# A two-layer attention trunk: when the sums for the output weights are taken, when the gates are scaled, and which engine splits the outputs

## The chip, the cores and the metric

The kernel runs on one core of one Trainium2 chip. The core has five engines with queues of their own: TensorE (PE, matrix products and transposes, with the loading of weights counted apart as PEld), VectorE (DVE), ScalarE (ACT), GpSimd (POOL) and SyncE (SP), which here issues every DMA. The metric is the device time of one launch in microseconds; the time of a kernel is the median of its runs.

## The reference, cut to what matters

A trunk of two layers over 1024 tokens of width 1024, 16 heads of 64, float32:

```python
for i in range(2):
    h = rmsnorm(x, norm_g[i])
    # layer 0: forgetting attention (causal, with a bias from cumulated log-gates)
    # layer 1: native sparse attention (compressed + selected blocks + sliding window, gated)
    o, z = mixer(h)                       # z is 1024 columns of the same input projection
    x = x + (o * silu(z)) @ w_out         # the output projection
out = rmsnorm(x, final_g)
```

What the change touches lies around the last line of the loop: the gate silu(z), the product with o, and the projection by W_out.

## The kernel before, in words

**Numbers.** TensorE multiplies in pairs of halves: a value is split into a high part and a rest (hi, lo), and a product is three matmuls, hi·hi, hi·lo, lo·hi (`mm3`, lines 256 to 258). The output projections do this in float16, so their operands are first scaled by powers of two. The scales come from bounds: a sum of squares of all of W_out, and for each pair of heads a sum of squares of z with a bound of v.

**Squares.** `Squares` (lines 160 to 187) holds a list of weight pieces. One `step` takes the square of the piece that was loaded last (ScalarE, L183, with its sum over each row) and then issues the load of the next (SyncE, L173). A tiny ScalarE operation (L182, tile `zg`) ties the step to some tile that has just been made, so that it comes at that place in the order. In layer 0 (`early`, one buffer) the steps stand behind each half of the k, v, q and z sections, and two behind each finished pair of the pairs 0 to 5. The list is 40 pieces of layer 1's input weights, then the gate weights (column 40 of `sums`), then 16 pieces of layer 0's W_out (columns 49 to 64).

**Order of the work.** Each layer runs two Python generators that `merge` interleaves by costs they yield: the main one is attention (scores, exponentials, transposes, products with v), the fill one is projections. Where one yields a function, it stands still until that condition holds. The order so traced is the priority of the instructions in each engine's queue; each engine then runs its own queue in order, and waits on semaphores for others.

In layer 0, `fox_fill` makes the sections k, v, q, z for eight pairs of heads, each section 8 steps of three 128x512 matmuls for each half of the tokens. `fox_main` works through duos of row blocks; the last duo of a pair calls the tail of `FoxDuo.finish`: transpose o (L793), multiply with the scale of the pair and z (L795), copy to float16 (ScalarE, L801), take the rest (GpSimd, L802), store (SyncE, L806). Pair 7 keeps its outputs on chip. In its turn in the fill come z, the second half of q, then `out_scales` (some 14 VectorE operations of a few elements, two ScalarE casts and two small matmuls, through `roots`), then the load of half of W_out, the first half of q, and the split of the rows. `load_wout16` splits W_out in pieces of 128x512: ScalarE makes the high part (L682); of every two pieces the rest of one is made by VectorE (L684) and of the other by GpSimd in two operations (L686, L687).

The scale of a pair in layer 0 is five VectorE operations on one column behind the second half of z (L574 to L577, with `half_root`, L222 and L224). In layer 1 it is seven (L1453 to L1459). `ready["c", p]` holds it.

In layer 1, `nsa_zs` is the fill: eight z sections of float16 matmuls, `out_scales`, the split of W_out, and products of finished pairs (`out_start`). The main part, `run_attn`, works through 32 `NsaSuper` (16 heads, two halves of the queries). For the window part of each, GpSimd makes the high half and the rest of the probabilities (L1628, L1629) and a transposing DMA (L1631) follows; the chosen blocks are transposed by TensorE (L1647) and split by ScalarE and VectorE (L273, L274). `close` does for layer 1 what the tail of `finish` does for layer 0 (L1704 to L1715).

At the end of either layer the rest of the fill runs as products only.

Of the kernel before, what the change touches and what calls it, by code (L numbers as in the profile page):

```python
# [21 lines left out]
P = 128  # L22
# [19 lines left out]
def tile_fox_nsa(ctx, tc, a, out):  # L42
# [409 lines left out]
    def fox_k(p):  # L452
        KH = [sk.tile([P, S], F32R, tag="KH", name=f"KH_{p}_{j}") for j in range(2)]
        KL = [sk.tile([P, S], F32R, tag="KL", name=f"KL_{p}_{j}") for j in range(2)]
        w = next_w() if p else wq.pop(0)
        for half in range(2):
            ts = slice(half * 512, half * 512 + 512)
            pt = ps_a(f"k{p}_{half}")
            yield from project(w, hT, half, pt)
            for j in range(2):  # L460
                r, o = rows[j], rows[1 - j]
                A.copy(KH[j][r, ts], pt[r, :])
                V.tensor_tensor(KL[j][r, ts], pt[r, :], f(KH[j][r, ts]), OP.subtract)
                dma(f(KH[j][o, ts]), f(KH[j][r, ts]))
                dma(f(KL[j][o, ts]), f(KL[j][r, ts]))
            yield 0
            if p:
                early.step(pt[:, 0:1])
        ready["k", p] = KH, KL
# [92 lines left out]
    def fox_z(p, w, halves=(1, 0)):  # L562
        zs = ready.setdefault(("zt", p), {})
        if not ao:
            ao.append(sb[0].tile([P, 8], F32, name="ao0", bufs=1))
        zq = sb[0].tile([P, 6], F32, tag="zq", bufs=3, name=f"zq_{p}")
        for half in halves:
            pt = ps_a(f"z{p}_{half}")
            yield from project(w, hT, half, pt)
            zs[half] = z = sb[0].tile([P, 512], F32, tag="z", bufs=4, name=f"z_{p}_{half}")  # L570
            A.activation(z, pt, AF.Square, accum_out=zq[:, half:half + 1])
            silu2(z, pt)
            if half == 0:
                V.tensor_tensor(zq[:, 2:3], zq[:, 0:1], zq[:, 1:2], OP.add)  # L574
                half_root(zq, 2)
                V.tensor_scalar(zq[:, 5:6], zq[:, 4:5], 2.0 ** 46, None, OP.mult)
                V.scalar_tensor_tensor(ao[0][:, p:p + 1], zq[:, 3:4], 2.0 ** 81, ready["v", p][1], OP.mult, OP.mult)  # L577
                ready["c", p] = zq[:, 5:6]
            ready["z", p, half] = zs
            early.step(z[:, 0:1])  # L580

    early = Squares(sa, [(a["nsa_w"][i][:, 4 * x:4 * x + 4, :], 2 * n + x)
                         for n, i in enumerate((*range(12), *range(20, 28))) for x in range(2)]
                    + [(a["nsa_w_g"].rearrange("(k p) c -> p k c", p=P), 40)] + row_sets(a["fox_w_out"], 512, 49), 512, 1)
    un0 = consts.tile([P, 12], F32, name="un0")
    ao = []
    first = []
# [1 line left out]
    def fox_fill():  # L589
        for p in range(8):  # L590
            if p >= 2:
                yield lambda p=p: ("scored", p - 2) in ready
            yield from k0 if p == 0 else fox_k(p)
            if p == 0:
                for _ in range(11):
                    yield next(gate0)
            if p >= 2:
                yield lambda p=p: ("done", p - 2) in ready
            yield from fox_v(p)
            if p == 0:  # L600
                yield from gate0
                sb.append(tc.alloc_tile_pool(name="sb", bufs=2, reuse_waits="tile"))
            if p < 7:
                yield from fox_q(p, next_w())
                yield from fox_z(p, next_w())
                if p == 6:
                    first.append(roots(sums[:, 0:41], ((0, 4), (4, 8), (8, 24), (24, 40), (40, 41)), "early"))
            else:
                wq, wz = next_w(), next_w()
                yield from fox_z(p, wz)  # L610
                yield from fox_q(p, wq, (1,))
                assert not early.items and not early.at
                ready["wscale"], ready["undo"] = out_scales(ao[0], sums[:, 49:65], "o0", un0, sb[0])
                rows0 = load_wout16(hp, "fox_w_out", 1, 200)
                yield next(rows0)
                yield from fox_q(p, wq, (0,))
                yield from rows0
                ready["o7"] = hp.tile([P, NT, 2, P], F16, tag="h11", name="o7_0")
                yield from out_start0(load_wout16(hp, "fox_w_out", 0, 200))

# [43 lines left out]
                load(n + 1)  # L664
                yield 1000

    def load_wout16(pool, src, half, pace, scale=None):


        lo = pool.tile([P, 4, D], F32, tag=f"h{half}1", name=f"wos_{src}_{half}")  # L670
        for k in range(4):
            r = 4 * (1 - half) + k
            dma(lo[:, k, :], a[src][r * P:(r + 1) * P, :])
        yield 0
        w = pool.tile([P, 2, 4, D], F16, tag=f"h{half}0", name=f"wo_{src}_{half}")
        for k in range(4):
            r = 4 * (1 - half) + k
            sc = ready["wscale"][:, r:r + 1]
            for c in range(2):
                yield pace  # L680
                cs = slice(c * 512, c * 512 + 512)
                A.activation(w[:, 0, k, cs], lo[:, k, cs], AF.Copy, scale=sc)  # L682
                if c:
                    V.scalar_tensor_tensor(w[:, 1, k, cs], lo[:, k, cs], sc, w[:, 0, k, cs], OP.mult, OP.subtract)  # L684
                else:
                    G.tensor_scalar(lo[:, k, cs], lo[:, k, cs], sc, 1.0, OP.mult, OP.mult)  # L686
                    G.tensor_tensor(w[:, 1, k, cs], lo[:, k, cs], w[:, 0, k, cs], OP.subtract)  # L687
        ready.setdefault("wout", []).append((w[:, 0], w[:, 1]))
# [7 lines left out]
    class FoxDuo:  # L696
# [78 lines left out]
        def finish(self):  # L775
# [10 lines left out]
            if j == 1 and x == 3:  # L786
                ready["done", p] = True
                for s in (1, 0):
                    yield lambda s=s: ("z", p, s) in ready
                    yield 1000  # L790
                    pt = ps_t(f"pto_{p}_{s}")
                    for i in range(4):
# [5 lines left out]
                    else:  # L798
                        ot = o[:, 4 * s:4 * s + 4].bitcast(F16).rearrange("p t (x q) -> p t x q", x=2)
                    z4 = z.rearrange("p (t q) -> p t q", t=4)  # L800
                    A.copy(ot[:, :, 0], z4)  # L801
                    G.tensor_tensor(ot[:, :, 1], z4, ot[:, :, 0], OP.subtract)  # L802
                    if p < 6:
                        early.step(z[:, 0:1])
                    if p < 7:
                        dma(oF[0][p * P:(p + 1) * P, 4 * s:4 * s + 4], ot)  # L806
                    ready["o", p, s] = True
# [615 lines left out]
    def limits():  # L1423
# [12 lines left out]
        V.tensor_scalar(b[:, 1].bitcast(I32), b[:, 0].bitcast(I32), 0x7F800000, None, OP.bitwise_xor)  # L1436
        ready["limits"] = b[:, 1]

    def nsa_z(p, w, halves=(1, 0)):
        if p == 0:  # L1440
            limits()
# [3 lines left out]
        zq = zs["q"]  # L1445
        for half in halves:
            pt = ps_a(f"nz{p}_{half}")
            yield from project(w, hT, half, pt)
            zs[half] = z = pers.tile([P, 512], F32, tag="z", bufs=4, name=f"nz_{p}_{half}")
            A.activation(z, pt, AF.Square, accum_out=zq[:, half:half + 1])  # L1450
            silu2(z, pt, ready["units"][2])
            if half == 0:
                V.tensor_tensor(zq[:, 2:3], zq[:, 0:1], zq[:, 1:2], OP.add)  # L1453
                half_root(zq, 2)
                V.tensor_scalar(zq[:, 5:6], zq[:, 4:5], 2.0 ** 74, None, OP.mult)
                V.tensor_tensor(zq[:, 6:7], zq[:, 5:6], ready["limits"][:, p // 2:p // 2 + 1], OP.mult)
                V.tensor_scalar(zq[:, 6:7], zq[:, 6:7], 2.0 ** 100, None, OP.min)
                V.tensor_scalar(zq[:, 7:8].bitcast(I32), zq[:, 6:7].bitcast(I32), 0x7F800000, None, OP.bitwise_xor)
                V.tensor_scalar(ao1[:, p:p + 1], zq[:, 7:8], 0.5, None, OP.mult)  # L1459
                ready["c", p] = zq[:, 6:7]  # L1460
                ready["z", p, 1] = zs
            if half == 0:
                ready["z", p, 0] = zs
            ready["v"] = True

    def nsa_zs():
        for p in range(8):
            if p == 6:
                rows0 = load_wout16(h1, "nsa_w_out", 1, 400)
                yield next(rows0)  # L1470
            if p >= 2:
                yield lambda p=p: ("done", p - 2) in ready
            yield from nsa_z(p, zw[p])
        assert not late.items and not late.at
        ready["wscale"], ready["undo"] = out_scales(ao1, late.out, "o1", pers.tile([P, 12], F32, name="un1"), pers)
        yield from rows0
        ready["o7"] = h1.tile([P, NT, 2, P], F16, tag="h11", name="o7_1")
        yield from out_start(load_wout16(h1, "nsa_w_out", 0, 400))

    class Halves:  # L1480

# [78 lines left out]
    class NsaSuper:  # L1560
# [134 lines left out]
        def close(self):  # L1695
# [2 lines left out]
            if h % 2 == 0:  # L1698
                return
            o, t = self.O[p, s], self.O[p, s, "t"]  # L1700
            yield lambda: ("z", p, s) in ready
            pt = ps_t(f"ptn_{self.name}")
            for qi in range(4):
                T.transpose(pt[:, qi * P:(qi + 1) * P], t[:, qi, :], ident)  # L1704
# [152 lines left out]
```

## Time and profile before

| | us |
|---|---|
| median of three runs | 1472.32 (1471.29 to 1477.2) |
| the profiled execution's own time | 1477.65 |
| its span, from first to last instruction | 1475.8 |
| TensorE busy | 1371.1 (93%) |
| VectorE busy | 1112.8 (75%) |
| ScalarE busy | 924.5 (63%) |
| GpSimd busy | 594.2 (40%) |

Layer 0 runs to about 620 us of the span (with its last products to about 655), the first part of layer 1 (projections, compressed attention, block choice) to about 980, sparse attention to about 1410, the end to 1476. A row of a wait view reads: who waited, for which engine and line, total us, times, the longest. A row of a group reads: line, engine, operation, tile out and in, shapes, count, then busy us and mean ns of one, then the engine's idle time before them and what ended it. A row of a tile view gives minimum, median and maximum ns and the first and last start in us.

### The profile page before, as it was taken

To read this page: it belongs to the slowest core of one execution; us is meant where nothing else is said; L and a number is where in the kernel's file an instruction comes from. 1 tells how busy PE (TensorE), PEld (TensorE's weight loads), DVE (VectorE), ACT (ScalarE), POOL (GpSimd) and SP (SyncE) were. 2 spreads that over 40 slices of the span, in tenths; PEclk is the share of its full clock that TensorE was granted. 3 is DMA by queue.
4 is the path that set the end of the run, shared out by engine and by line. 5 is a ranking of instruction groups with operands and counts; after the bars stand their busy time and mean duration, and the time that the engine had idled before them with its cause. 6 is when DMAs were issued, how large, how long until landed. Compare 5 with 4: busy or idle time off the path is not lost. (4 is left out here: it accounts for less than half of the span.)

```text
span 1475.8 us, 30392 instructions
## 1 busy us (share of the span) xinstructions
PE 1371.1 (93%) x10499; PEld 931.0 (63%) x10499; DVE 1112.8 (75%) x3010; ACT 924.5 (63%) x2344; POOL 594.2 (40%) x785
## 2 busy tenths in 40 slices
PE   5999999999999989989999988879999999988998
PEld 4878877877777755444545544447666766655643
DVE  6586677776868788586757667878989999888834
ACT  5376767676776564255555476657877878778612
POOL 2233333323332352121202456235766766669500
PEclk9999999999999999999999999999999999999999
DMA  5388788887988898546464446445667686774633
GB/s 200 90 174 187 186 186 198 193 187 190 188 197 169 162 260 193 118 154 198 140 222 124 152 110 164 121 137 100 123 147 167 134 175 123 145 173 100 120 113 143
DMA packets 414923, 234.73 MB, mean 159 GB/s; under 512 B 334448, under 2 KB 372656, under 8 KB 414768
## 3 DMA queue, kind: packets, MB, share of 16 engines
q1 hardware_dynamic: 414768, 232.78, 66.5%
q8 instruction: 83, 1.36, 0.4%
q14 instruction: 72, 0.59, 0.1%
HBM read 120.31 MB, written 28.38 MB: 101 GB/s over the span
## 5 line engine op out<-in xcount | busy, mean ns | idle before, releaser
L1614 PE MATMUL S_n<-nk,nq 128*128 128x320 f16 (+5 forms) x768 | 156.8, 318 | 17.4 <-DVE m_n L1622 16.1
L755 ACT ACTIVATE P<-P,m 128x512 f32<-128x512 f32 (+1 forms) x192 | 116.3, 607 | 56.3 <-DVE m L746 55.5
L1629 POOL TENSOR_TENSOR hl_n<-P_n,hl_n 128x640 f16<-128x640 f32 (+4 forms) x128 | 143.8, 1123 | 10.0
L757 DVE SCALAR_TENSOR_TENSOR hl<-P,hl 128x512 f16<-128x512 f32 (+1 forms) x192 | 115.3, 616 | 41.2 <-ACT hl L756 39.9
L726 POOL TENSOR_TENSOR Bd<-B,tri 128x128 f32<-128x128 f32 x128 | 61.6, 498 | 203.0 <-DVE m L746 187.0
L1628 POOL CAST hl_n<-P_n 128x640 f16<-128x640 f32 (+4 forms) x128 | 76.8, 600 | 116.2 <-ACT P_n L1625 91.5
L1625 ACT ACTIVATE P_n<-P_n,m_n 128x640 f32<-128x640 f32 (+7 forms) x128 | 98.5, 770 | 32.2 <-DVE m_n L1622 31.3
L1625 ACT ACTIVATE P_n<-P_n,m_n,units 128x640 f32<-128x640 f32 (+4 forms) x128 | 100.1, 783 | 28.7 <-DVE m_n L1624 25.6
L1614 PEld LDWEIGHTS <-nq 128*128 128x128 f16 x768 | 71.8, 99 | 63.7 <-issue 27.3
L273 ACT ACTIVATE pth_n<-ptp_n 128x512 f16<-128x512 f32 (+1 forms) x160 | 85.4, 545 | 40.4 <-PE ptp_n L1647 39.1
L274 DVE SCALAR_TENSOR_TENSOR ptl_n<-ptp_n,pth_n 128x512 f16<-128x512 f32 (+1 forms) x160 | 99.9, 633 | 11.1 <-ACT pth_n L273 8.8
L1647 PE MATMUL ptp_n<-ident,P_n 128*128 128x128 f32 x576 | 94.3, 281 | 5.3 <-DVE un L238 1.7
L756 ACT ACTIVATE hl<-P 128x512 f16<-128x512 f32 (+1 forms) x192 | 92.6, 512 | 2.0 <-ACT P L755 0.4
L1622 DVE CUSTOM_DVE_ANT_0 P_n<-S_n,wmask 128x640 f32<-128x640 f32 (+4 forms) x128 | 83.2, 650 | 9.0 <-PE S_n L1614 8.8
L183 ACT ACTIVATE sq<-sq,zg 128x512 f32<-128x512 f32 (+2 forms) x73 | 59.5, 815 | 39.7 <-DMA sq<-in_nsa_w_dram 24.8
L1647 PEld LDWEIGHTS ptp_n<-ident,P_n 128*128 128x128 f32 x576 | 66.3, 143 | 27.5 <-DVE ptl_n L274 9.3
L1622 DVE CUSTOM_DVE_ANT_0 P_n<-S_n,bias,units 128x640 f32<-128x640 f32 (+1 forms) x64 | 68.8, 1075 | 4.6 <-PE S_n L1614 4.6
L771 PE MATMUL O<-v,pT 128*128 128x128 f16 x576 | 59.4, 223 | 13.7 <-DMA pT<-hl 9.8
L1655 PE MATMUL O_n<-nv,pth_n 128*128 128x64 f16 x576 | 71.7, 193 | 0.2
L1656 PE MATMUL O_n<-nv,pth_n 128*128 128x64 f16 x576 | 71.7, 193 | 0.0
L737 PE MATMUL S<-KH,Q 128*128 128x512 f32 (+1 forms) x192 | 66.3, 360 | 3.7 <-DVE m L746 2.2
L1657 PE MATMUL O_n<-nv,ptl_n 128*128 128x64 f16 x576 | 68.8, 193 | 0.3 <-DVE ptl_n L274 0.3
(522 smaller groups left out, 4707.2 us busy)
## 6 DMA issues: line engine op xcount, KB each, us to landing
sq<-in_nsa_w_dram SPq DMA_DIRECT2D x40, 256.0 KB
B<-cD SPq DMA_DIRECT2D x16, 512.0 KB
nq<-qD SPq DMA_DIRECT2D x64, 128.0 KB
x<-in_x_dram SPq DMA_DIRECT2D x8, 512.0 KB
wst_k<-in_fox_w_dram SPq DMA_DIRECT2D x8, 512.0 KB
wst_v<-in_fox_w_dram SPq DMA_DIRECT2D x8, 512.0 KB
wst_q<-in_fox_w_dram SPq DMA_DIRECT2D x8, 512.0 KB
KH<-KH SPq DMA_DIRECT2D x32, 128.0 KB
```

Of the source, the lines that this page charges most:

```text
L273: A.activation(hi[:, 0:n], pt[:, 0:n], AF.Copy, scale=scale)
L274: V.scalar_tensor_tensor(lo[:, 0:n], pt[:, 0:n], scale, h, OP.mult, OP.subtract)
L755: A.activation(L[:, 0:n], L[:, 0:n], AF.Exp, bias=init, scale=-1.0, accum_out=self.lr[:, col + c:col + c + 1])
L756: A.activation(hi[:, cs], L[:, 0:n], AF.Copy, scale=UP)
L757: V.scalar_tensor_tensor(lo[:, cs], L[:, 0:n], UP, hi[:, cs], OP.mult, OP.subtract)
L1614: T.matmul(ps[:, b, 0:w], self.q[x][:, qi * P:(qi + 1) * P], k[:, k0 + b * w:k0 + b * w + w], start=(x == 0), stop=(x == 1))
L1622: V.tensor_tensor_reduce(dst, src, mk, 1.0 if y else unit, 3e38, OP.add, OP.min, m)
L1625: A.activation(L, L, AF.Exp, bias=m, scale=minus if y else -1.0, accum_out=self.l[:, y, qi:qi + 1])
L1628: G.tensor_copy(hl[:, 0:n], L)
L1629: G.tensor_tensor(hl[:, n:2 * n], L, hl[:, 0:n], OP.subtract)
L1647: T.transpose(pt[:, (x + i) * P:(x + i + 1) * P], L[:, kb * P - k0:(kb + 1) * P - k0], ident)
L1655: T.matmul(o, hi, v[:, 0:64], start=first, stop=False)
```

## The change

1. `early` takes the 16 pieces of W_out before the gate weights, and no longer has steps behind finished pairs. Its last step now stands behind the last half of the last pair's q.
2. The scale of pair p in layer 0 moves into `z_scale`, called behind the first half of pair p+1's k section; for pair 7 behind the second half of q. `finish` waits for the scale instead of z.
3. In layer 0's last pair `out_scales` moves behind the load of W_out's rows and four steps of the first half of q; the roots of layer 1's weights move from the end of pair 6 to behind the split of the rows.
4. The float16 copy in `finish` moves from ScalarE to GpSimd.
5. In layer 1 the scale moves into `nz_scale`, called four steps into the next pair's z section, for pair 7 behind a pause of 2000 cost units; `out_scales` follows it. `close` waits for the scale.
6. In layer 1 `load_wout16` gets `gp=False`: the rests are all made by VectorE.

```diff
@@ fox_k
             yield from project(w, hT, half, pt)
+            if p and half == 0:
+                z_scale(p - 1)
@@ fox_z (nsa_z likewise loses its seven operations at half 0)
             silu2(z, pt)
-            if half == 0:
-                V.tensor_tensor(zq[:, 2:3], zq[:, 0:1], zq[:, 1:2], OP.add)
-                half_root(zq, 2)
-                V.tensor_scalar(zq[:, 5:6], zq[:, 4:5], 2.0 ** 46, None, OP.mult)
-                V.scalar_tensor_tensor(ao[0][:, p:p + 1], zq[:, 3:4], 2.0 ** 81, ready["v", p][1], OP.mult, OP.mult)
-                ready["c", p] = zq[:, 5:6]
...
+    def z_scale(p):
...
@@ early
-                    + [(a["nsa_w_g"].rearrange("(k p) c -> p k c", p=P), 40)] + row_sets(a["fox_w_out"], 512, 49), 512, 1)
+                    + row_sets(a["fox_w_out"], 512, 49)
+                    + [(a["nsa_w_g"].rearrange("(k p) c -> p k c", p=P), 40)], 512, 1)
@@ fox_fill
-                if p == 6:
-                    first.append(roots(sums[:, 0:41], ..., "early"))
             else:
                 wq, wz = next_w(), next_w()
                 yield from fox_z(p, wz)
                 yield from fox_q(p, wq, (1,))
-                ready["wscale"], ready["undo"] = out_scales(ao[0], sums[:, 49:65], "o0", un0, sb[0])
+                z_scale(p)
                 rows0 = load_wout16(hp, "fox_w_out", 1, 200)
                 yield next(rows0)
-                yield from fox_q(p, wq, (0,))
+                last_q = fox_q(p, wq, (0,))
+                for _ in range(4):
+                    yield next(last_q)
+                ready["wscale"], ready["undo"] = out_scales(ao[0], sums[:, 49:65], "o0", un0, sb[0])
+                yield from last_q
                 yield from rows0
+                first.append(roots(sums[:, 0:41], ..., "early"))
@@ load_wout16
-                if c:
+                if c or not gp:
                     V.scalar_tensor_tensor(w[:, 1, k, cs], lo[:, k, cs], sc, w[:, 0, k, cs], OP.mult, OP.subtract)
@@ FoxDuo.finish
-                    yield lambda s=s: ("z", p, s) in ready
+                    yield lambda: ("c", p) in ready
...
-                    A.copy(ot[:, :, 0], z4)
+                    G.tensor_copy(ot[:, :, 0], z4)
                     G.tensor_tensor(ot[:, :, 1], z4, ot[:, :, 0], OP.subtract)
-                    if p < 6:
-                        early.step(z[:, 0:1])
@@ nsa_z
+            steps = project(w, hT, half, pt)
+            if half and p:
+                for _ in range(4):
+                    yield next(steps)
+                nz_scale(p - 1)
+            yield from steps
@@ nsa_zs
-                rows0 = load_wout16(h1, "nsa_w_out", 1, 400)
+                rows0 = load_wout16(h1, "nsa_w_out", 1, 400, False)
...
+        yield 2000
+        nz_scale(7)
         ready["wscale"], ready["undo"] = out_scales(ao1, late.out, ...)
...
-        yield from out_start(load_wout16(h1, "nsa_w_out", 0, 400))
+        yield from out_start(load_wout16(h1, "nsa_w_out", 0, 400, False))
@@ NsaSuper.close
-            yield lambda: ("z", p, s) in ready
+            yield lambda: ("c", p) in ready
```

More of the change, by code (lines that the diff above doesn't have):

```diff
@@ L565, in fox_z @@
             ao.append(sb[0].tile([P, 8], F32, name="ao0", bufs=1))
-        zq = sb[0].tile([P, 6], F32, tag="zq", bufs=3, name=f"zq_{p}")
+        zs["q"] = zq = sb[0].tile([P, 6], F32, tag="zq", bufs=3, name=f"zq_{p}")
         for half in halves:
@@ L572, in fox_z @@
             silu2(z, pt)
-            if half == 0:
-                V.tensor_tensor(zq[:, 2:3], zq[:, 0:1], zq[:, 1:2], OP.add)
-                half_root(zq, 2)
-                V.tensor_scalar(zq[:, 5:6], zq[:, 4:5], 2.0 ** 46, None, OP.mult)
-                V.scalar_tensor_tensor(ao[0][:, p:p + 1], zq[:, 3:4], 2.0 ** 81, ready["v", p][1], OP.mult, OP.mult)
-                ready["c", p] = zq[:, 5:6]
             ready["z", p, half] = zs
             early.step(z[:, 0:1])
+    def z_scale(p):
+        zq = ready["zt", p]["q"]
+        V.tensor_tensor(zq[:, 2:3], zq[:, 0:1], zq[:, 1:2], OP.add)
+        half_root(zq, 2)
+        V.tensor_scalar(zq[:, 5:6], zq[:, 4:5], 2.0 ** 46, None, OP.mult)
+        V.scalar_tensor_tensor(ao[0][:, p:p + 1], zq[:, 3:4], 2.0 ** 81, ready["v", p][1], OP.mult, OP.mult)
+        ready["c", p] = zq[:, 5:6]
     early = Squares(sa, [(a["nsa_w"][i][:, 4 * x:4 * x + 4, :], 2 * n + x)
                          for n, i in enumerate((*range(12), *range(20, 28))) for x in range(2)]
-                    + [(a["nsa_w_g"].rearrange("(k p) c -> p k c", p=P), 40)] + row_sets(a["fox_w_out"], 512, 49), 512, 1)
+                    + row_sets(a["fox_w_out"], 512, 49)
+                    + [(a["nsa_w_g"].rearrange("(k p) c -> p k c", p=P), 40)], 512, 1)
     un0 = consts.tile([P, 12], F32, name="un0")
@@ L605, in fox_fill @@
                 yield from fox_z(p, next_w())
-                if p == 6:
-                    first.append(roots(sums[:, 0:41], ((0, 4), (4, 8), (8, 24), (24, 40), (40, 41)), "early"))
             else:
@@ L611, in fox_fill @@
                 yield from fox_q(p, wq, (1,))
-                assert not early.items and not early.at
-                ready["wscale"], ready["undo"] = out_scales(ao[0], sums[:, 49:65], "o0", un0, sb[0])
+                z_scale(p)
                 rows0 = load_wout16(hp, "fox_w_out", 1, 200)
                 yield next(rows0)
-                yield from fox_q(p, wq, (0,))
+                last_q = fox_q(p, wq, (0,))
+                for _ in range(4):
+                    yield next(last_q)
+                assert len(early.at) == 1 and not early.items
+                ready["wscale"], ready["undo"] = out_scales(ao[0], sums[:, 49:65], "o0", un0, sb[0])
+                yield from last_q
                 yield from rows0
+                assert not early.at
+                first.append(roots(sums[:, 0:41], ((0, 4), (4, 8), (8, 24), (24, 40), (40, 41)), "early"))
                 ready["o7"] = hp.tile([P, NT, 2, P], F16, tag="h11", name="o7_0")
@@ L665, in out_start0, with load_wout16 @@
                 yield 1000
-    def load_wout16(pool, src, half, pace, scale=None):
+    def load_wout16(pool, src, half, pace, gp=True):
         lo = pool.tile([P, 4, D], F32, tag=f"h{half}1", name=f"wos_{src}_{half}")
@@ L1437, in limits, with nz_scale @@
         ready["limits"] = b[:, 1]
+    def nz_scale(p):
+        zq = ready["zt", p]["q"]
+        V.tensor_tensor(zq[:, 2:3], zq[:, 0:1], zq[:, 1:2], OP.add)
+        half_root(zq, 2)
+        V.tensor_scalar(zq[:, 5:6], zq[:, 4:5], 2.0 ** 74, None, OP.mult)
+        V.tensor_tensor(zq[:, 6:7], zq[:, 5:6], ready["limits"][:, p // 2:p // 2 + 1], OP.mult)
+        V.tensor_scalar(zq[:, 6:7], zq[:, 6:7], 2.0 ** 100, None, OP.min)
+        V.tensor_scalar(zq[:, 7:8].bitcast(I32), zq[:, 6:7].bitcast(I32), 0x7F800000, None, OP.bitwise_xor)
+        V.tensor_scalar(ao1[:, p:p + 1], zq[:, 7:8], 0.5, None, OP.mult)
+        ready["c", p] = zq[:, 6:7]
     def nsa_z(p, w, halves=(1, 0)):
@@ L1447, in nsa_z @@
             pt = ps_a(f"nz{p}_{half}")
-            yield from project(w, hT, half, pt)
+            steps = project(w, hT, half, pt)
[4 more added lines that the diff above has]
+            yield from steps
             zs[half] = z = pers.tile([P, 512], F32, tag="z", bufs=4, name=f"nz_{p}_{half}")
@@ L1451, in nsa_z @@
             silu2(z, pt, ready["units"][2])
[L1452 to L1463, printed above, removed]
+            ready["z", p, half] = zs
             ready["v"] = True
```

## The prediction

> **What bounds the kernel now.** I read the busy shares of the page first, then the busy time of every engine stage by stage, then TensorE's waits in the two places that the change touches, then single tiles and lines.
>
> The page gives TensorE (PE) 93% and VectorE (DVE) 75%. The stage table, with its boundaries set by hand, says where this is not true. Its columns are busy microseconds with the instruction count, then TensorE's granted clock, the DMA engines' busy share and GB/s.
>
> ```profile
> span 1475.8 us, 30392 instructions
> PE 1371.1 (93%) x10499; PEld 931.0 (63%) x10499; DVE 1112.8 (75%) x3010; ACT 924.5 (63%) x2344; POOL 594.2 (40%) x785
> ...
> core 0: us, PE busy (x) PEld busy (x) DVE busy (x) ACT busy (x) POOL busy (x), PEclk, DMA share, GB/s
> 60.00:440.00 380.00, 369.76 (x2244) 297.85 (x2243) 275.44 (x875) 263.14 (x703) 129.90 (x202) 1.00 0.84 187
> 512.00:562.00 50.00, 42.75 (x262) 26.42 (x261) 43.12 (x123) 31.43 (x75) 22.38 (x27) 0.90 0.98 239
> 980.00:1310.00 330.00, 313.15 (x3973) 222.04 (x3973) 295.90 (x822) 254.12 (x597) 215.47 (x257) 0.99 0.70 142
> 1310.00:1362.00 52.00, 41.35 (x460) 28.15 (x459) 44.26 (x123) 40.77 (x87) 41.96 (x44) 0.93 0.50 120
> 1362.00:1400.00 38.00, 36.75 (x488) 26.10 (x487) 31.89 (x85) 25.20 (x59) 22.41 (x28) 1.00 0.68 134
> ...
> 1100.00:1200.00 100.00, 95.70 (x1241) 68.37 (x1240) 91.81 (x254) 78.54 (x185) 67.43 (x80) 1.00 0.73 154
> ...
> 1420.00:1430.00 10.00, 10.00 (x48) 4.49 (x47) 0.00 (x0) 0.00 (x0) 0.00 (x0) 1.00 0.01 3
> ```
>
> The long part of layer 0 (60 to 440) has TensorE busy 369.76 of 380 us: work taken from ScalarE (ACT) or GpSimd (POOL) is worth nothing there unless it ends one of the few holes. The two poor stretches are 512 to 562 (last pair's queries, scales and split of W_out in layer 0; DMA engines 98% busy) and 1310 to 1362 (the same step in layer 1). In the second TensorE idles 10.65 us of 52, where the stage before idles 16.85 of 330, or 5.1%.
>
> What TensorE waited for, first from 60 to 620, then from 1317 to 1362 (total us, times, longest):
>
> ```profile
> PE O L771 <- DMA pT<-hl: 9.8, 4, 2.9
> PE pto L793 <- DVE o L785: 2.9, 1, 2.9
> PE O L771 <- ACT zg L182: 2.5, 1, 2.5
> ...
> PE S_n L1614 <- DVE m_n L1622: 4.1, 5, 1.4
> PE ptn_n L1704 <- POOL ot_n L1691: 3.1, 2, 1.6
> PE ptp_n L1647 <- DVE un L238: 1.7, 1, 1.7
> PE y L257 <- POOL wo_nsa_w_out L687: 1.4, 2, 0.8
> ```
>
> A hole also lowers the clock. These rows are the stretch right behind the 2.5 us hole, and the one around the holes of layer 1:
>
> ```profile
> 234.00:237.40 3.40, 3.40 (x13) 2.73 (x11) 1.25 (x5) 1.89 (x6) 0.46 (x1) 0.51 1.59 248
> 1323.00:1329.60 6.60, 5.21 (x21) 2.99 (x19) 4.91 (x29) 4.44 (x14) 4.51 (x8) 0.50 0.90 245
> ```
>
> At half clock the busy time there is twice what the work needs: 3.4 / 2 = 1.7 us behind the first hole, 5.21 / 2 = 2.6 us in layer 1. So the most that layer 1's part can give is 10.65 - 0.051 x 52 = 8.0, plus 2.6: 10.6 us. The Trainium skill ("TensorE: Matmul & The Clock Gate", Part 1: The HAM clock gate) has the clock fall after an idle window of about 3.4 us; by that alone no hole here would cost more than itself, and layer 1 could give 8.0. The trace disagrees: the longest waits in the two lists are 2.9 and 1.7 us, and the clock fell all the same, so the measured 10.6 stands.
>
> **The change part by part.** Rows that carry the prices:
>
> ```profile
> L801 ACT CAST o<-z x16: 602/617/620, 149.4 to 617.0; 128x512 f16<-128x512 f32 x16
> L802 POOL TENSOR_TENSOR o<-z,o x16: 1154/1164/1172, 150.1 to 617.7; 128x512 f16<-128x512 f32 x16
> L1628 POOL CAST hl_n<-P_n 128x512 f16<-128x512 f32 x16 | 10.2, 640 | 17.7 <-ACT P_n L1625 17.7
> SPq L806 <- POOL o L802: 12.9, 8, 3.1
> L183 ACT ACTIVATE sq<-sq,zg x57: 617/724/728, 73.6 to 456.4; 128x512 f32<-128x512 f32 x56, 128x384 f32<-128x384 f32 x1
> SPq L173 <- ACT sq L183: 15.4, 17, 2.0
> DMA packets 23221, 13.21 MB, mean 232 GB/s; under 512 B 19376, under 2 KB 21424, under 8 KB 23216
> L198 DVE TENSOR_REDUCE roots_early<-total_early x5: 146/163/165, 466.9 to 467.2; 128x1 f32<-128x4 f32 x2, 128x1 f32<-128x16 f32 x2, 128x1 f32<-128x1 f32 x1
> L574 DVE TENSOR_TENSOR zq<-zq x8: 151/496/707, 88.5 to 513.6; 128x1 f32<-128x1 f32 x8
> L1453 DVE TENSOR_TENSOR nzq<-nzq x8: 155/159/1261, 979.1 to 1318.6; 128x1 f32<-128x1 f32 x8
> L684 DVE SCALAR_TENSOR_TENSOR wo_fox_w_out<-wos_fox_w_out,un,wo_fox_w_out x8: 725/840/1726, 530.9 to 559.4; 128x512 f16<-128x512 f32 x8
> L684 DVE SCALAR_TENSOR_TENSOR wo_nsa_w_out<-wos_nsa_w_out,un,wo_nsa_w_out x8: 733/762/1195, 1332.0 to 1367.1; 128x512 f16<-128x512 f32 x8
> L686 POOL TENSOR_SCALAR wos_nsa_w_out<-wos_nsa_w_out,un x8: 688/946/1203, 1331.3 to 1349.7; 128x512 f32<-128x512 f32 x8
> L687 POOL TENSOR_TENSOR wo_nsa_w_out<-wos_nsa_w_out,wo_nsa_w_out x8: 1155/1162/1718, 1332.0 to 1351.0; 128x512 f16<-128x512 f32 x8
> ```
>
> *Outputs of layer 0 split by GpSimd alone.* Sixteen ScalarE copies of 0.617 us go (9.9 us), sixteen GpSimd casts come, at the 0.640 of the same shape in layer 1 (10.2 us). The chain from z to its store gets 0.02 us longer and loses one hand-over between engines. Behind the waiting GpSimd instruction stand Bd, which VectorE needs for the next scores, and the low halves of the next weights, as they stood behind the subtraction before; SyncE (SP), which waited 12.9 us in all for these splits before its stores, waits the same within 0.02 us a time. TensorE's 369.76 of 380 covers both engines: 0. Uncovered it would be 16 x 0.64 = 10 us on GpSimd, of which I keep 1 as the bound, since GpSimd is busy 34% there (129.90 of 380); the other bound is -1.
>
> *Squares.* The 57 squares are the same; 12 of the 70 places where one can be taken go (two behind each of the pairs 0 to 5), so 58 places are left for 57 squares and the first load. The last square moves from 456 us to the last pair's last query half, near 537. Gain: squares come less bunched. The one place where bunching reached TensorE is here, three squares within 13 us, each waiting for its own load:
>
> ```profile
> 224.54 0.73 ACT L183 ACTIVATE sq<-sq,zg 128x512 f32<-128x512 f32 x1 [1.68 <-DMA sq<-in_nsa_w_dram]
> 228.01 0.72 ACT L183 ACTIVATE sq<-sq,zg 128x512 f32<-128x512 f32 x1 [0.76 <-DMA sq<-in_nsa_w_dram]
> 233.03 0.17 ACT L182 ACTIVATE zg<-k 128x1 f32<-128x1 f32 x1 [1.36 <-DVE KL L463]
> ```
>
> The third row is what the 2.5 us wait of O was for: the PSUM tile of k is freed only when ScalarE has read it. The middle square is one of the removed ones. If this hole goes, 2.5 + 1.7 = 4.2 us; I take half, -2, since the next bunch may fall elsewhere (bounds -4.2 and 0). Cost: the late squares load in 505 to 523, where the DMA engines are full. Two sets of 256 KB at 239 GB/s are 1.1 us each. The gate weights come in 1024 pieces of 192 bytes; from 505 to 562, 23221 packets took 57 us at a busy share of 0.98, 2.4 ns each over all engines, so 2.4 us. Together 4.6 us, ahead of or between W_out's rows and the transposes of P, for which TensorE already waited 9.8 us in four places. On SyncE each square's load waits 0.9 us (15.4 / 17) for the square before it, with transposes behind. I take +2.5 (bounds 0, and 4.6 plus one more 2.9 us hole with two half-clock windows, 3.4: 10.9). The roots of these sums move too: five reductions of 0.16 and two small operations, 1.1 us of VectorE, with one small matmul, from 467 into 512 to 562, where VectorE is busy 43.12 of 50. Take +0.5, bounds 0 and 1.1.
>
> *Scales of z a section later.* No instruction is added: five small ones a pair in layer 0, seven in layer 1. The first of them took 0.496 in layer 0 where 0.151 is its least, so 8 x 0.35 = 2.8 us of VectorE could go, under a TensorE that is busy 97%: 0 (bounds -1, 0). The new wait, for the scale in place of z, is traced a whole section before a pair is finished, and what would queue behind it on TensorE are the four transposes of the pair's output: 0 (bounds 0 and 0.5). In layer 0 the scales of W_out come four projection steps later, behind the same row loads: 0, with +-1 for the 0.1 to 0.2 us operations landing elsewhere.
>
> *Layer 1: scales later, W_out split on VectorE.* GpSimd loses eight pairs of 0.946 + 1.162, 16.9 us of the 41.96 that it is busy in 1310 to 1362. That ends the waits for ot_n (3.1) and wo (1.4). VectorE gains 8 x 0.762 = 6.1 us. Some of its present 44.26 us is stretched (L1453 above took 1.26 us where 0.159 is usual); I take 2 us off. Over 1310 to 1400 its work is 44.26 + 31.89 + 6.1 - 2 = 80.3 us; at the 89.7% it reaches from 980 to 1310 that is 89.5 us, and at the 91.8% of 1100 to 1200 it is 87.5, where 90 are spent now. So VectorE, not GpSimd, is late next, and it caps the gain. Take -2.5. Bounds: -10.6, all excess idle gone, and (44.26 + 6.1) / 0.897 - 52 = +4.1, nothing made up in the next stretch. The pause of 2000 units moves 3.1 projection steps (650 units and three matmuls each), at 10 / 48 = 0.21 us a matmul some 1.9 us of TensorE work, into the stretch that ends in pure matmul work (48 in 10 us): free where TensorE is the bound (36.75 of 38), at most +1.9; take 0.
>
> Sum: -2 + 2.5 + 0.5 - 2.5 = -1.5. Against the profiled execution's own 1477.65 us (span 1475.8 and 1.85 around it) that is 1476.2. That execution lies 5.3 us above the median, 1472.32; the same -1.5 there gives 1470.8, which I give as 1470.5.
>
> **The rivals.** *All holes close.* The layer 1 stretch returns to 5.1% idle at full clock (-10.6), the hole at 231 goes (-4.2), the late loads cost nothing: 1472.3 - 14.8 = 1457.5. For it: GpSimd is busy 41.96 of the 52 us, and loses 16.9. Against: VectorE's 6.1 us more.
>
> *VectorE is held up by GpSimd.* In layer 0 the same split took up to 1.726 us beside GpSimd's, against 0.725. If all eight new ones take that, 13.8 us, then (44.26 + 13.8) / 0.897 = 64.7, 12.7 us more than now: 1485. It decides (7.4 us slower) from 9.0 us of added VectorE time, 53.3 in all. Against: GpSimd's own share, the likely cause, leaves. The Trainium skill ("SBUF — State Buffer", Who interferes with whom) says that a VectorE instruction with two SBUF inputs contends with a GpSimd instruction that reads SBUF; by that rule the new splits, which read wos and the high half, would meet the window casts and subtractions that stay, as this rival has it; the 1.726 agrees with it.
>
> *Late loads open a hole in layer 0.* 10.9 us at 512 to 562 less 2.5 gained in layer 1: 1480.7. For it: DMA share 0.98 there. Against: TensorE has the last query half to work on.
>
> That the change does nothing that can be measured is the forecast itself.
>
> **How the numbers follow.** A difference of 0.5% (7.4 us) is about what a measurement of this kernel can tell from none. Forecast 0.54 (own range 1465 to 1479), all holes close 0.22, held-up VectorE 0.10, late loads 0.14. The range, 1459 to 1482, leaves out half of the first rival and most of the second. Faster 0.22, same 0.54, slower 0.24.
>
> **What would show it.** Waits of TensorE for ot_n and wo_nsa_w_out gone, VectorE at 90% or more of 1310 to 1400, GpSimd near 25 us busy in 1310 to 1362: right. L684 above 1.2 us on average in layer 1: the second rival. More than 10 us of waits for pT, or ScalarE's wait for the rows of W_out longer, before 620: the third. Wrong also if holes in parts of layer 0 that the change hardly touches move the sum by more than 5 us.

## The result, and the profile after

| | median, us | runs |
|---|---|---|
| before | 1474.76 | 1471.29 to 1477.6 |
| after | 1461.13 | 1459.79 to 1461.67 |

The ratio is 0.9907 (0.988 to 0.9935): 13.6 us faster, where 1.5 were forecast. The time lies inside the range and outside the likeliest case's own range; the gain comes from another place than the one where the rival "all holes close" had most of it. The page of the changed kernel:

```profile
span 1458.8 us, 30392 instructions
...
PE 1364.8 (94%) x10499; PEld 928.3 (64%) x10499; DVE 1119.4 (77%) x3018; ACT 915.7 (63%) x2328; POOL 588.2 (40%) x785
```

TensorE's 10499 instructions are the same, its busy time is 6.3 us less: fewer of them ran at half clock. Where the time went is read from stretches of the same work, from the first half of the first q to the start of the last pair's z. Stage table of the kernel before, then of the one after:

```profile
59.16:496.70 437.54, 424.34 (x2570) 341.85 (x2568) 319.59 (x1018) 297.87 (x795) 148.35 (x230) 0.99 0.84 185
```

```profile
58.75:477.41 418.66, 417.84 (x2570) 339.36 (x2568) 321.56 (x1009) 286.53 (x759) 158.09 (x242) 1.00 0.87 189
...
60.00:440.00 380.00, 379.30 (x2336) 308.29 (x2335) 292.50 (x921) 263.03 (x695) 142.28 (x220) 1.00 0.86 190
```

The same 2570 TensorE instructions take 437.54 us before and 418.66 after: 18.9 us less. TensorE's idle time falls from 437.54 - 424.34 = 13.2 us to 0.8, which is 12.4; its busy time falls by 6.5, the clock. So the whole gain, and more, arises in the long part of layer 0, which the prediction's stage table had shown as nearly full (369.76 of 380). Less of it remains at the end: the profiles as wholes differ by 17.0 us, because the changed kernel takes 2.3 us longer behind this part, and the medians by 13.6, because the profiled execution before was 2.9 us above its median. The holes there before, from 60 to 440, and the only one after:

```profile
PE O L771 <- ACT zg L182: 2.5, 1, 2.5
PE z L256 <- DVE Q L558: 1.7, 2, 0.9
PE S L737 <- DVE m L746: 1.3, 4, 0.7
PE O L771 <- DMA pT<-hl: 1.3, 1, 1.3
PE S L737 <- DVE Q L558: 1.0, 1, 1.0
PE O L771 <- DVE ot L783: 1.0, 2, 0.6
PE v L256 <- DVE ot L783: 0.9, 1, 0.9
PE O L771 <- ACT vT L538: 0.4, 1, 0.4
```

```profile
PE S L748 <- DVE m L757: 0.7, 1, 0.7
```

Only one of the eight rows before names the squares' line; all eight went. One engine further up, ScalarE's waits for the loads of its squares in the same 380 us, before:

```profile
ACT sq L183 <- DMA sq<-in_nsa_w_dram: 24.8, 14, 4.3
ACT sq L183 <- DMA sq<-in_fox_w_out_dram: 10.7, 7, 2.8
ACT sq L183 <- DMA sq<-in_nsa_w_g_dram: 2.9, 1, 2.9
```

and after:

```profile
ACT sq L183 <- DMA sq<-in_nsa_w_dram: 9.0, 8, 2.1
ACT sq L183 <- DMA sq<-in_fox_w_out_dram: 4.2, 2, 2.5
```

They fall from 38.4 to 13.2 us. VectorE stands between the two: its waits for ScalarE, before and then after:

```profile
DVE hl L757 <- ACT hl L756: 33.9, 29, 4.5
DVE KL L463 <- ACT KH L462: 18.2, 10, 6.6
```

```profile
DVE hl L768 <- ACT hl L767: 15.7, 26, 1.4
...
DVE KL L465 <- ACT KH L464: 7.5, 8, 3.2
```

The longest single waits for hl and KL were 4.5 and 6.6 us, and are 1.4 and 3.2. So a TensorE hole put down to VectorE's Q or to a transposed P can have begun at a square; the experiments below test that.

The last stage loses some of it. From the last score of layer 1 to the end, stage table of before, then of after:

```profile
1396.39:1475.79 79.40, 71.72 (x444) 35.12 (x442) 35.69 (x68) 18.48 (x50) 6.41 (x7) 0.98 0.38 123
```

```profile
1376.65:1458.78 82.13, 73.93 (x453) 36.01 (x452) 36.60 (x69) 18.66 (x50) 6.72 (x8) 0.98 0.40 124
...
1292.00:1382.00 90.00, 79.55 (x947) 55.23 (x945) 79.84 (x217) 65.07 (x147) 48.74 (x56) 0.96 0.62 127
1296.00:1348.00 52.00, 43.40 (x504) 30.74 (x503) 46.49 (x130) 40.46 (x91) 27.16 (x32) 0.93 0.64 140
1310.00:1362.00 52.00, 43.75 (x530) 30.49 (x527) 48.28 (x128) 37.71 (x83) 26.17 (x29) 0.97 0.53 117
```

The end is 2.7 us longer and has nine more matmuls in it, three steps of projection. The other three rows are taken up below. The first is the prediction's 1310 to 1400 moved forward by 18 us, to nearly the same work (947 matmuls beside 948). The second is 1310 to 1362 moved forward by 14 us, as the splits of W_out are, and holds 44 matmuls more. The third is 1310 to 1362 as it stands.

### The profile page after: what moved, and what is told of

The parts are those of the page before. It is cut to its first block, busy times and chain, and to the rows that moved or that the text cites. A ratio compares the mean times of both kernels' runs of the same rounds, so it can differ in the third digit from the quotient of the medians.

```text
span 1458.8 us, 30392 instructions
## 1 busy us (share of the span) xinstructions
PE 1364.8 (94%) x10499; PEld 928.3 (64%) x10499; DVE 1119.4 (77%) x3018; ACT 915.7 (63%) x2328; POOL 588.2 (40%) x785
## 5 line engine op out<-in xcount | busy, mean ns | idle before, releaser
L1643 ACT ACTIVATE P_n<-P_n,m_n,units 128x640 f32<-128x640 f32 (+4 forms) x128 | 100.1, 782 | 24.5 <-DVE m_n L1642 23.8
L97 ACT ACTIVATE h_n<-xr 128x512 f32<-128x512 f32 x32 | 20.0, 626 | 81.6 <-DVE xr L1765 39.2
```

The costliest lines, as they stand in the source:

```text
L1643: A.activation(L, L, AF.Exp, bias=m, scale=minus if y else -1.0, accum_out=self.l[:, y, qi:qi + 1])
```

## The experiments

Each set of runs timed the kernel before anew, so a difference between kernels of two sets is taken from each one's own kernel before. Two accounts were set against each other for the gain in layer 0. The first: ScalarE works through its queue in order, a square whose load was issued too late holds everything behind it, and VectorE and TensorE follow. The second: the copies taken from ScalarE did it.

**The squares alone, on the kernel before.**

```diff
-    + [gate weights] + row_sets(a["fox_w_out"], 512, 49), 512, 1)
+    + row_sets(a["fox_w_out"], 512, 49) + [gate weights], 512, 1)
...
-                    if p < 6:
-                        early.step(z[:, 0:1])
```

(with the roots of layer 1's weights at their later place)

> The kernel before, with only the squares changed: W_out's pieces ahead of the gate weights, no steps behind finished pairs, the roots of layer 1's weights behind the split of the rows. Theory 1 (bunched squares: ScalarE stood still behind the loads of squares, freed PSUM late, and TensorE had holes): ScalarE's wait for square loads from 60 to 440 falls from 38.4 us to about 13, the last pair's z section starts about 19 us earlier, and the median is 10 to 16 us below before. Theory 2 (the float16 copy on ScalarE, which waits in order for z, made the holes): nothing moves before the last pair, median within 3 us of before.

1461.86 us beside 1474.21: 0.992 (0.9896 to 0.9945), -12.3 us. Its stage row and ScalarE's waits from 60 to 440:

```profile
60.00:440.00 380.00, 379.26 (x2335) 308.15 (x2335) 291.88 (x918) 269.21 (x704) 136.25 (x210) 1.00 0.86 189
```

```profile
ACT sq L183 <- DMA sq<-in_nsa_w_dram: 8.7, 6, 2.0
ACT sq L183 <- DMA sq<-in_fox_w_out_dram: 3.0, 2, 2.5
```

The holes from 60 to 440 close as in the changed kernel, with the copies still on ScalarE (704 instructions against 695).

**The copy on GpSimd alone, on the kernel before.**

```diff
-                    A.copy(ot[:, :, 0], z4)
+                    G.tensor_copy(ot[:, :, 0], z4)
```

> The kernel before, with only the float16 copy of layer 0's outputs moved to GpSimd. Theory 1: the median stays within 3 us of before, and the hole of 2.5 us near 231 stays. Theory 2: the last pair's z section starts about 19 us earlier, the median is 10 us or more below before.

1471.78 us, 0.9988 (0.9974 to 1.0002): no difference that can be told. From 60 to 440:

```profile
60.00:440.00 380.00, 370.94 (x2249) 298.80 (x2248) 276.49 (x878) 259.62 (x697) 136.54 (x212) 1.00 0.83 188
```

TensorE stays at 371 us. The second account falls.

**The changed kernel with the squares as before** (the reverse of the first edit).

> The changed kernel with the squares as they were: gate weights ahead of W_out, steps behind finished pairs, roots at pair 6. Theory 1: the holes of layer 0 come back, ScalarE's wait for square loads from 60 to 440 is 30 us or more, the last pair's z section starts less than 6 us earlier than before, the median is 8 to 14 us above the changed kernel. Theory 2, or a theory 3 that the later scales of z did it: the median stays within 3 us of the changed kernel.

1470.97 us, 0.9985 (0.9971 to 1.0): all of the change but the squares is worth 3.2 us at the median, and at most 0.3%. TensorE's row is back:

```profile
60.00:440.00 380.00, 369.87 (x2249) 297.83 (x2249) 278.98 (x878) 260.26 (x697) 136.91 (x212) 1.00 0.84 188
```

**The parts of layer 1 alone, on the kernel before:** `nz_scale`, the pause, `close` waiting for the scale, and W_out split on VectorE.

> The kernel before, with only layer 1's parts: later scales, the pause of 2000 units, W_out split on VectorE alone. From the two traces the stretch from the first window score to the last lost 1.4 us and the tail behind it gained 2.8, so the parts of layer 1 cost about 1 us together: median 0 to 3 us above before. By the prediction's step for layer 1 it would be 2.5 us below, by its second rival 10 or more above.

1474.95 us, 1.001 (0.9996 to 1.0024): +0.7. What the waits of the changed kernel show there stands below. Here too TensorE is busy only 369.21 of the 380 us in layer 0: the four profiles with squares and buffers as before have 369 to 371, all seven with the squares moved have 379.3.

**Two buffers for the squares, on the kernel before.** If late loads are the cause, loading one piece ahead should help with the steps left where they were. To make room for the second buffer of 256 KB, one of the two staging tiles for the split v, of the same size, was given up.

```diff
-    ... + row_sets(a["fox_w_out"], 512, 49), 512, 1)
+    ... + row_sets(a["fox_w_out"], 512, 49), 512, 2)
+    early.load()
...
-    tag="vs", bufs=2, name=f"vs_{p}_{half}"
+    tag="vs", bufs=1, name=f"vs_{p}_{half}"
```

> The kernel before with all its 70 places for squares, but two buffers for their loads, so that a square's load is issued a step earlier (room for it comes from one buffer instead of two for the split v). Theory 1a (ScalarE waiting for loads that were issued too late made the holes): ScalarE's wait for square loads from 60 to 440 falls below 10 us, TensorE is busy more than 377 of 380 us there, the last pair's z section starts 12 to 20 us earlier, median 8 to 15 us below before. Theory 1b (the steps behind finished pairs tie ScalarE to the pair's output, whatever the loads do): TensorE stays near 370 of 380 and the median within 3 us of before.

1471.8 us, 0.9981 (0.9968 to 0.9993): only -3.4, and TensorE is busy 371.90 of the 380 us, where the first account expected more than 377. ScalarE's waits from 60 to 440:

```profile
ACT vs L544 <- DMA v<-vs: 15.9, 6, 5.6
ACT sq L183 <- DMA sq<-in_fox_w_out_dram: 5.7, 5, 1.6
ACT sq L183 <- DMA sq<-in_nsa_w_dram: 5.0, 5, 1.5
```

The waits for squares did fall, to 10.7 us, but the tile given up brought 15.9 us of a new wait of the same kind. By itself this run decides nothing; it needs a control.

**One staging tile for v, alone, on the kernel before** (the second edit of the run above without the first).

> The control of the two-buffer run: the kernel before with one buffer instead of two for the split v, and nothing else. In that run ScalarE's wait for the split v's store (15.9 us) and a 3.7 us hole at 136 us were new. If the smaller v buffer made them, the control has them too, its last pair's z section starts 5 to 8 us later than before, and two buffers for squares are worth the difference of the two runs, 8 to 12 us. If the control equals before, two buffers are worth only the 3.4 us measured, and theory 1a explains a quarter of the gain.

1489.6 us beside 1473.2, 1.0117 (1.01 to 1.0134): +16.4, and TensorE is busy only 359.65 of the 380 us. ScalarE's waits:

```profile
ACT sq L183 <- DMA sq<-in_nsa_w_dram: 25.5, 14, 4.3
ACT vs L544 <- DMA v<-vs: 16.4, 6, 5.5
...
ACT sq L183 <- DMA sq<-in_fox_w_out_dram: 7.0, 4, 3.0
ACT sq L183 <- DMA sq<-in_nsa_w_g_dram: 2.7, 1, 2.7
```

Against this control the second buffer is worth 16.4 + 3.4 = 19.8 us, give or take some 3 by the two intervals, each kernel taken against the kernel before of its own set; 8 to 12 were expected. TensorE gains 12.2 us of busy time in the 380. For this 35.2 - 10.7 = 24.5 us of waits for squares went: 0.8 us of time for each us. The changed kernel has 18.9 us of layer 0 for 25.2 us, 0.75. So the first account holds by two routes: moving the steps apart, and loading ahead with the steps left where they were. The price is no constant, though. The wait for the staging tile, of another kind, came out dearer (16.4 us of it, beside 3.2 less for squares, for 16.4 of time), and a long wait behind 471 us in the changed kernel cost TensorE nothing (under the copies below).

**W_out's pieces first in the list, on the changed kernel,** so that the square taken last belongs to layer 1 and `out_scales` need not wait for it.

```diff
-    early = Squares(sa, [layer 1's 40 pieces] + row_sets(a["fox_w_out"], 512, 49) + [gate weights], 512, 1)
+    early = Squares(sa, row_sets(a["fox_w_out"], 512, 49) + [layer 1's 40 pieces] + [gate weights], 512, 1)
```

> The changed kernel with W_out's squares first in the list, so that the last squares are of layer 1's weights, which the scales of W_out don't need. If the 2.9 us hole at the small matmul of W_out's total (with half a clock window of 3.4 us behind it) is due to the last W_out square waiting 3.4 us for its load, the hole goes and the median is 2 to 5 us below the changed kernel. If the place of the scales' small matmuls in TensorE's order is enough for a hole, the median stays within 2 us.

1459.72 us, 0.9905 (0.9881 to 0.9928): 1.8 less than the changed kernel, each beside its own kernel before, which the intervals don't separate. The 2.9 us wait at `total_o0w` is gone, but from 440 to 620 this row takes its place, one of its three waits 4.6 us long:

```profile
PE O L782 <- DMA pT<-hl: 7.3, 3, 4.6
```

**The changed kernel without the pause of 2000 units** (the line `yield 2000` removed).

> The changed kernel without layer 1's pause of 2000 units. If the pause pushed matmuls into the tail, the tail from the last window score to the end is about 2 us shorter; if the pause keeps the scales' chain clear of TensorE, 1 to 3 us of new holes come at the scales instead. Median within 3 us of the changed kernel either way; the trace tells.

1457.59 us, 0.9886 (0.9869 to 0.9904): 3.9 less than the changed kernel, each beside its own kernel before. From the last score to the end:

```profile
1379.10:1458.50 79.40, 71.73 (x445) 35.10 (x442) 35.71 (x68) 18.48 (x50) 6.41 (x7) 0.99 0.37 122
```

The tail has its 79.40 us and 445 TensorE instructions again. Two of the waits that the pause had removed or shortened come back from 1296 to 1348:

```profile
PE S_n L1631 <- DVE m_n L1639: 3.9, 4, 1.4
PE ptp_n L1664 <- DVE un L238: 1.7, 1, 1.7
```

In exchange the 3.7 us wait for a load of queries, which the changed kernel has there (below), is gone.

**Layer 1's W_out split by VectorE and GpSimd again, on the changed kernel** (the two `False` arguments removed).

> The changed kernel with layer 1's W_out split between VectorE and GpSimd as before. By the prediction's step (GpSimd's 16.9 us filled the stretch) the waits of TensorE for ot_n and for W_out come back and the median is 1 to 4 us above the changed kernel. If VectorE's 6.1 us cost as much as GpSimd's freed time gave, it stays within 1 us.

1463.25 us, 0.9922 (0.9907 to 0.9937): 1.7 more than the changed kernel, each beside its own kernel before, of the sign expected and not separated by the intervals. VectorE's half of the splits, and TensorE's waits from 1290 to 1350:

```profile
L695 DVE SCALAR_TENSOR_TENSOR wo_nsa_w_out<-wos_nsa_w_out,un,wo_nsa_w_out x8: 743/1129/1711, 1319.4 to 1353.0; 128x512 f16<-128x512 f32 x8
```

```profile
PE S_n L1632 <- DMA nq<-qD: 4.7, 1, 4.7
PE ptn_n L1722 <- POOL ot_n L1709: 2.8, 2, 1.8
```

The wait for ot_n is back. Beside GpSimd's share VectorE's split has a median of 1.129 us.

**Both: W_out's pieces first, and no pause.**

> The changed kernel with W_out's squares first in the list and without layer 1's pause. The two runs of one of these each were 1.4 and 3.5 us below the changed kernel; if they add, the median is 1455 to 1458. If the holes only move, it stays at 1457.5 to 1461.

1455.83 us (1454.93 to 1458.71), 0.9888 (0.9873 to 0.9902): the fastest of all, 17.4 us under the kernel before of its set. Taking the pause away is worth 1.9 us here and 3.9 above, each kernel beside its own kernel before. The intervals overlap within each pair; the two pairs agree in sign. The tail shows it more plainly: from the start of the last score to the end, the five profiled kernels with the pause take 82.5 to 82.6 us and the eight without it 79.7 to 79.8.

**The same, with layer 0's W_out split on VectorE alone as well** (`False` in both of layer 0's calls of `load_wout16`).

> The run before this in the list, with layer 0's W_out also split on VectorE alone. Layer 1's split on VectorE alone was worth 2.1 us. If GpSimd's two operations a piece are what TensorE waits for (3.5 us for W_out in the changed kernel), the median is 1 to 4 us lower than the run with GpSimd; if VectorE, busy 45.56 of 50 us there, is the bound, it is 0 to 5 us higher.

1461.41 us, 0.9922 (0.9907 to 0.9937): 5.6 more than without that edit. From 500 to 620:

```profile
PE S L748 <- DVE m L757: 4.0, 3, 3.3
```

The waits for GpSimd's splits go and TensorE waits for VectorE's scores in their place. The step that seems to help layer 1 a little hurts layer 0.

## Why the prediction was right and wrong

**Squares: the step that failed.** It took -2, between -4.2 and 0. The first experiment takes in the late loads and the roots too, for which the sum had +2.5 and +0.5, so +1.0 in all; it measured -12.3 (by the interval, -8 to -15). The mechanism was named rightly, squares bunched behind single loads, each with its own wait. The error was the sentence that the one place where bunching reached TensorE was the hole put down to ScalarE. It priced 2.5 us of about 10 us of holes from 60 to 440, and one drop of the clock, since the other rows of that list name VectorE or a DMA. The first experiment closed those too, with only the squares and the roots touched. The rows with 38.4 us of ScalarE waiting for squares were there to be read and were not priced; at the 0.8 measured by the two-buffer pair, the 25.2 us that went would have been 20, and layer 0's long part gave 18.9. The prediction had named, as a sign of being wrong, holes that move the sum by more than 5 us in parts of layer 0 that the change hardly touches. Holes of layer 0 did move it by more, but in the part that the moved squares reach.

**Roots moved.** Not measured apart; +0.5 is inside what the first experiment took in.

**Late square loads: the hole came, another way round.** ScalarE waits for a late square, the last square and its cast for the sums of W_out follow, and TensorE stands for the cast. The changed kernel's timeline of ScalarE, then of TensorE, and the clock behind:

```profile
500.68 0.72 ACT L183 ACTIVATE sq<-sq,zg 128x512 f32<-128x512 f32 x1 [3.44 <-DMA sq<-in_fox_w_out_dram]
509.09 0.19 ACT L194 CAST sb_o0w<-sums 128x16 bf16<-128x16 f32 x1
```

```profile
509.33 0.17 PE L196 MATMUL total_o0w<-sb_o0w,ones 128*128 128x16 bf16 x1 [2.92 <-ACT sb_o0w L194]
```

```profile
509.70:513.10 3.40, 3.40 (x24) 2.69 (x23) 2.57 (x16) 2.33 (x6) 0.00 (x0) 0.51 1.15 284
```

The run with W_out's pieces first has such a wait of ScalarE at the same place (3.2 us), but its cast needs no late square and the hole is gone: it was the sum's dependence on the last square that reached TensorE. 2.9 us and 1.7 of half clock are 4.6, inside 0 to 10.9 and above the +2.5 taken. The prediction had placed the cost at W_out's rows and the transposes. Neither grew: waits for pT were 3.0 us in one place before 620, against 9.8 in four, and ScalarE's 6.3 us wait for the rows of W_out, there before, is gone (it waits 10.5 us for late squares instead, from 440 to 620). So the third rival's 10.9 us hole did not come.

**Copies on GpSimd, and z's scales:** 0 each. With the squares as before, 0.9988 and 0.9985 are hardly distinct from 1, as forecast. With the squares moved, where the copy runs does matter, which the prediction did not see. In the run with the squares alone ScalarE waits 6.8 us for a square's load, until 479.55. The copy, still on ScalarE, stands behind it; GpSimd's subtraction waits for the copy, the low halves of z's weights stand behind the subtraction, and TensorE waits for them:

```profile
480.95 1.16 POOL L802 TENSOR_TENSOR o<-z,o 128x512 f16<-128x512 f32 x1 [7.70 <-ACT o L801]
483.86 0.79 PE L258 MATMUL z<-hT,wlo_z 128*128 128x512 f32 x1 [4.77 <-POOL wlo_z L134]
```

In the changed kernel ScalarE waits 6.6 us at the same place, with the copy on GpSimd, and TensorE's wait for these low halves is 0.2 us; it is 0.2 in all six profiles with both parts of the change. What this is worth in the median was not measured by itself.

**Layer 1: its steps as described, its sum not.** The waits from 1296 to 1348 of the changed kernel:

```profile
PE S_n L1632 <- DMA nq<-qD: 3.7, 1, 3.7
PE S_n L1632 <- DVE m_n L1640: 2.3, 5, 1.1
PE ptp_n L1665 <- ACT P_n L1643: 1.4, 2, 1.0
```

```profile
L695 DVE SCALAR_TENSOR_TENSOR wo_nsa_w_out<-wos_nsa_w_out,un,wo_nsa_w_out x16: 702/743/1212, 1317.8 to 1353.3; 128x512 f16<-128x512 f32 x16
```

The waits for ot_n and for W_out went, and GpSimd is busy 26.17 us in 1310 to 1362 (27.16 in the stretch moved forward), where 25 were forecast. VectorE has 79.84 of 90 us (88.7%), just under the 90% said. But a wait of 3.7 us for a load of queries came, which the prediction did not see. It comes with the pause: it is 3.2 to 4.9 us in all five profiles with the pause, and at most 0.6 in the eight without. Idle time stayed 8.6 of 52 us (43.40 busy) where 10.65 were before. The forecast was -2.5; alone, the parts measure +0.7 together (-0.6 to +3.5 by the interval). The pause is the term that was mis-sized: "free where TensorE is the bound, at most +1.9", taken as 0, and it costs about 2 to 4. Its three projection steps were counted rightly (nine matmuls); the tail they were pushed into grew by 2.7 us for 2.2 of TensorE work. What the wait for queries adds to that, and what the holes closed by the pause take off, was not measured apart. The split on VectorE is worth some -2, near the -2.5, and is not clear of the noise. The second rival falls: the median split took 0.743 us, not 1.726. "All holes close" had the time nearly right and the place wrong: it had 10.6 of its 14.8 us in layer 1, and 4.2 at the hole at 231. So the time lies inside the range by luck: the range reached that low for a gain that was placed in layer 1.

The sum of the measured groups: -12.3 (squares) and -3.2 (all else) make -15.5, beside -13.6 with an interval of -9.6 to -17.7.

**Left open.** How the pause brings about the wait for queries, and where the 4.6 us wait for pT comes from, was not tried.

## What to carry to other kernels

When an engine runs in order, count its idle time before instructions that wait for a DMA, wherever the bound engine's wait list points: here a us of ScalarE waiting for squares cost about 0.8 us on average in the long part of layer 0, while TensorE's own list put 2.9 of some 10 us of holes down to ScalarE. A one-buffer prefetch tied to steps at uneven distances makes its engine wait where two steps stand close; spread the steps or load one ahead, and before judging a run that had to give something else up for the second buffer, run what was given up alone. A pause that moves filler work past its cover lengthens the uncovered tail, here by 2.7 us, even where it closes the holes that it was placed at.

## What the runs showed of the hardware

The clock fell to about half behind a 2.92 us hole (0.51 for 3.4 us at 509.7), as the prediction's row had it behind 2.5. VectorE's split beside GpSimd's has a median of 1.129 us in layer 1 of the run with GpSimd's share put back, and 0.743 in the changed kernel without that share. The Trainium skill ("SBUF — State Buffer", Who interferes with whom) has a VectorE instruction with two SBUF inputs contend with a GpSimd instruction that reads SBUF; that run agrees by these 0.39 us. In the kernel before the same split had a median of only 0.762 us beside GpSimd's, whose L686 took up to 1.203 us there with 0.688 as its least, so there the delay seems to fall on GpSimd instead. Lastly, code that was not touched varies: layer 0 is the same in the kernel before and in the run with layer 1's parts alone, and its first window score starts at 971.5 us in the one profile and at 967.8 in the other, so a difference of under 4 us over that long a stretch says nothing in two single profiles, while the tail repeats within 0.1 us. The scores' rows, of the kernel before and of that run:

```profile
L1614 PE MATMUL S_n<-nk,nq x768: 216/299/634, 971.5 to 1396.0; 128*128 128x320 f16 x80, 128*128 128x384 f16 x32, 128*128 128x512 f16 x32, 128*128 128x448 f16 x16
```

```profile
L1623 PE MATMUL S_n<-nk,nq x768: 216/299/581, 967.8 to 1390.0; 128*128 128x320 f16 x80, 128*128 128x384 f16 x32, 128*128 128x512 f16 x32, 128*128 128x448 f16 x16
```
